# A fused attention and recurrence block: the query split and the gate's scaling move to GpSimd, the gated product reads PSUM, queries are scaled at their projection, and pieces are re-timed

## The chip, the cores and the metric

One Trainium2 chip; the program runs on one of its cores. The metric is the device time of one execution in microseconds (us), the median of several runs. Engines are named as the profile names them: PE is TensorE (PEld its weight loads), DVE VectorE, ACT ScalarE, POOL GpSimd, SP the queue that issues the transfers.

## The reference

2048 tokens of 1024 channels, float32. Eight attention heads of 128 channels with a forget bias, and a gated recurrence beside them; both are normed, gated and multiplied by one output matrix, then a second gate is added. The attention branch, which the change touches, is:

```python
xn = rmsnorm(h, pre_gain[i])
z = xn @ w_in[i]
q, k, v, fl, g_attn, x_lru, g_lru = jnp.split(z, SPLIT_POINTS, axis=-1)
# per head, causal, c = cumsum(log_sigmoid(fl + b_f)):
s = jnp.einsum('bhqd,bhkd->bhqk', qi, k) * HEAD_DIM ** -0.5
s = s + (ci[:, :, :, None] - c[:, :, None, :])
w = jax.nn.softmax(s, axis=-1)            # masked above the diagonal
o = jnp.einsum('bhqk,bhkd->bhqd', w, v)
y_attn = rmsnorm(o_attn, attn_out_gain[i]) * jax.nn.silu(g_attn)
...
mix = jnp.concatenate([y_attn, y_lru], axis=-1) @ w_out[i]
```

## The kernel before

Every product of matrices is made of three matmuls (`mm3`, lines 65 to 70): each operand is split into a high half, rounded to the matmul's format, and a low half, the rest; high x high, high x low and low x high are summed in a PSUM bank. `split` (line 47) makes the halves: ACT or another engine copies, DVE or POOL subtracts.

There are three stages. In the first the projections are made and written to memory: keys `kT_d`, queries `qT_d`, values `v_d`, gates `gT_d`. `plan_pair` makes two 512-row blocks of a pair of projections with seven products of half the size; `sum_` adds each finished bank to a running tile on DVE (line 375), and the last sums of a key and query unit (kind "k") are the queries, named "o" and "t2".

The second stage is attention. Its order is written out by hand: time is cut in slots, and `before` and `after` hold the work that is issued at the begin and the end of a slot; `at(before, slot, f)` puts it there, and each engine works through its own instructions in that order. A unit is a head h and a group g of 512 query rows. Group g has 4g + 4 key blocks and takes as many slots, so that a head has 4 + 8 + 12 + 16 = 40 slots; `t0[n]` is the first slot of unit n, and the boundary between two heads lies at t0 of a group 0. In a slot TensorE issues, in this order: the scores of a later unit (into one of three PSUM banks `sbank`), the value products of three slots before (`AHEAD`; into `obank`), and the transposes of one key block's probabilities (into `tbank`). In the last three slots of a unit a key block touches only some of the four query blocks, so the transposes and value products there are narrower.

What the other engines do for it:

- DVE reads a score bank, adds the forget bias (`bias`, or `dg` at the diagonal) and takes the running minimum `m` (line 1298); the bank is free when this is done. ACT takes the exponential (line 1307).
- ACT and DVE split the transposed probabilities into `th` and `tl` (lines 54 and 60).
- The next unit's queries are loaded into `qf` and split into `qh` (ACT, line 1235) and `ql` (DVE, line 1237) by `split_u`, four to seven slots before its first scores.
- The next head's keys and values come in eight pieces of 512 rows (`kvf`, three buffers), even ones keys, odd ones values: `load_piece` issues the transfer, `split_piece` makes `kh`, `vh` on ACT and `kl`, `vl` on POOL.
- `spread_sums` brings the inverse sums of the exponentials to all partitions (`rb`, line 1363). When a unit's value products are done, `finish_unit` forms `on` = bank x `rb` (line 1367), `gate_unit` forms `gs` = `on` x gate (line 1370), both on DVE, and POOL adds the squares of `on` to `acca` (lines 1377 to 1380).
- POOL also adds the causal mask to `dg` (line 1153) and does chores of the third stage (`make_t`, line 1496; `scale_l`, line 1479).

In the last head the output weights (`wst`) are loaded and split on ACT and POOL as well. The third stage makes the output products.

Of the kernel before, what the change touches and what calls it, by code (L numbers as in the profile page):

```python
# [9 lines left out]
F32 = mybir.dt.float32  # L10
F32R = mybir.dt.float32r
AF = mybir.ActivationFunctionType
ALU = mybir.AluOpType
# [3 lines left out]
P = 128  # L17
# [3 lines left out]
KD = D // P  # L21
# [3 lines left out]
BIG = 3.0e38  # L25
QSCALE = 128.0 ** -0.5
# [12 lines left out]
LOAD, COMBINE, PREP, JOB, MUL, GATE, STORE = range(7)  # L39
# [8 lines left out]
def f32(ap):  # L48
    return ap.bitcast(F32)


def split(nc, src, hi, lo, eh, el):
    if eh == "act":
        nc.scalar.activation(hi, src, AF.Copy)  # L54
    elif eh == "dve":
        nc.vector.tensor_copy(hi, src)
    else:
        nc.gpsimd.tensor_copy(hi, src)
    eng = nc.vector if el == "dve" else nc.gpsimd
    eng.tensor_tensor(out=lo, in0=src, in1=f32(hi), op=ALU.subtract)  # L60


def mm3(nc, out, ws, xs, start, stop):


    wh, wl = ws
    xh, xl = xs
    nc.tensor.matmul(out, lhsT=wh, rhs=xh, start=start, stop=False)  # L68
    nc.tensor.matmul(out, lhsT=wh, rhs=xl, start=False, stop=False)  # L69
    nc.tensor.matmul(out, lhsT=wl, rhs=xh, start=False, stop=stop)  # L70
# [3 lines left out]
def hymba_kernel(ctx: ExitStack, tc: tile.TileContext, x, xT, pT, w_p, w_v, w_o, w_ple, w_pg,  # L74
                 w_gates, vecs, rows, mgrp, out):
    nc = tc.nc
# [37 lines left out]
    rstd_a = const.tile([P, TB], F32, name="rstd_a")  # L114
# [48 lines left out]
    def pool_(stack, name, bufs=1, side="left", space=None):  # L163
        kw = {"side": side} if space is None else {"side": side, "space": space}
        return stack.enter_context(tc.tile_pool(name=name, bufs=bufs, reuse_waits="tile", **kw))


    def scaled_split(q, hi, lo):
        nc.scalar.activation(hi, q, AF.Copy, scale=QSCALE)
        nc.vector.scalar_tensor_tensor(out=lo, in0=q, scalar=QSCALE, in1=f32(hi), op0=ALU.mult, op1=ALU.subtract)  # L170

    p1 = ctx.enter_context(ExitStack())
    ps1 = ctx.enter_context(ExitStack())
    kvA_stack = ctx.enter_context(ExitStack())
# [13 lines left out]
    rs_x = xp.tile([P, TB], F32, name="rs_x")  # L188
    zf = xp.tile([P, NH, TB], F32, name="zf")
    carry = xp.tile([P, NH], F32, name="carry")  # L190
    ps = pool_(ps1, "ps1", 2, space=PSUM)
    pairs_stack = ps1.enter_context(ExitStack())
    wide = [pool_(pairs_stack, "pairs", 3, space=PSUM), None]
# [4 lines left out]
    def bank():  # L198
        return wide[1].tile([P, 512], F32, name="bank", bufs=6)
# [5 lines left out]
    def sbank():  # L205
        return ps.tile([P, 512], F32, name="sbank", bufs=2)

    def ctile():
        return ep.tile([P, 512], F32, name="c", bufs=NC)
# [3 lines left out]
    def plan(slot, phase, f):  # L213


        assert (slot, phase) >= tuple(now), (slot, phase, now)
        order_[0] += 1
        heapq.heappush(calendar.setdefault(slot, []), (phase, order_[0], f))
# [155 lines left out]
    def add(o, x, y):  # L374
        nc.vector.tensor_tensor(out=o, in0=x, in1=y, op=ALU.add)  # L375

    def plan_pair(u, done):


        b, T = u.begin, {}  # L380

        def mul(i):
            T[i] = bank()
            wh, wl, _ = u.ops[i, 0]
            for k in range(4):
                ks = slice(k * P, (k + 1) * P)
                mm3(nc, T[i], (wh[:, ks], wl[:, ks]), (XH[i][:, k], XL[i][:, k]), k == 0, k == 3)

        def copy(name, src):
            T[name] = ctile()  # L390
            nc.scalar.activation(T[name], T[src], AF.Copy)

        def sum_(name, x, y):
            if name not in T:
                T[name] = ctile()
            add(T[name], T[x], T[y])

        for m, i in enumerate(u.order):
            plan(b + m, MUL, lambda i=i: mul(i))

        plan(b + 1, COMBINE, lambda: copy("t1", 0))
        plan(b + 2, COMBINE, lambda: sum_("t2", 2, "t1"))
        plan(b + 3, COMBINE, lambda: sum_("t1", 5, "t1"))
        plan(b + 4, COMBINE, lambda: sum_("t5", 1, "t2"))
        plan(b + 6, COMBINE, lambda: sum_("o", 4, "t5"))
        plan(b + 6, COMBINE, lambda: sum_("t2", 4, "t2"))
        plan(b + 7, COMBINE, lambda: sum_("t5", 3, "t5"))
        plan(b + 7, COMBINE, lambda: sum_("t2", 6, "t2"))
        done(u, 0, 0, T, "t1", b + 3)
        done(u, 1, 1, T, "o", b + 6)  # L410
        done(u, 0, 1, T, "t5", b + 7)
        done(u, 1, 0, T, "t2", b + 7)
# [404 lines left out]
    b = sbank()  # L817
# [128 lines left out]
    for i in range(8):  # L946
        h, c = jobs.pop(0)
# [30 lines left out]
    for i in range(24):  # L978
        h, c = jobs.pop(0)
# [87 lines left out]
    parts_ = {}  # L1067
# [33 lines left out]
    def q_split(g):  # L1101
        qh = kvA_[0].tile([P, 512], F32R, name=f"qh{g}", bufs=1)
        ql = kvA_[0].tile([P, 512], F32R, name=f"ql{g}", bufs=1)
        scaled_split(parts_.pop(("q", g)), qh, ql)
        early_q[g] = qh, ql

    def first_masks():
# [72 lines left out]
    def load_piece(h, n):  # L1180
        c = n // 2
        f = ap.tile([P, 4, P], F32, name="kvf", bufs=3)
        if n % 2 == 0:
            nc.sync.dma_start(out=f.rearrange("p a b -> p (a b)"), in_=kT_d[h, :, c * 512:(c + 1) * 512])
        else:
            nc.sync.dma_start(out=f, in_=v_d[h, :, c * 4:c * 4 + 4])
        pieces[h, n] = f

    def split_piece(h, n):
        if n == 0:  # L1190
            s = Ctx()
            kv = kvB if h % 2 else kvA
            s.kh = kv.tile([P, S], F32R, name="kh")
            s.kl = kv.tile([P, S], F32R, name="kl")
            s.vh, s.vl = {}, {}
            heads[h] = s
        s = heads[h]
        f = pieces.pop((h, n))
        c = n // 2
        if n % 2 == 0:  # L1200
            cs = slice(c * 512, (c + 1) * 512)
            split(nc, f.rearrange("p a b -> p (a b)"), s.kh[:, cs], s.kl[:, cs], "act", "pool")
        else:
            bs, a = slice(c % 2 * 4, c % 2 * 4 + 4), c // 2
            if c % 2 == 0:
                kv = kvB if h % 2 else kvA
                s.vh[a] = kv.tile([P, 8, P], F32R, name=f"vh{a}")
                s.vl[a] = kv.tile([P, 8, P], F32R, name=f"vl{a}")
            split(nc, f, s.vh[a][:, bs], s.vl[a][:, bs], "act", "pool")
# [21 lines left out]
    def split_u(u, part):  # L1231
        if part == 0:
            u.qh = ap.tile([P, 512], F32R, name="qh", bufs=2)
            u.ql = ap.tile([P, 512], F32R, name="ql", bufs=2)
            nc.scalar.activation(u.qh, u.qf, AF.Copy, scale=QSCALE)
        else:
            nc.vector.scalar_tensor_tensor(out=u.ql, in0=u.qf, scalar=QSCALE, in1=f32(u.qh),
                                           op0=ALU.mult, op1=ALU.subtract)

    p1.close()  # L1240
    ps1.close()
# [9 lines left out]
    def load_w(n, k):  # L1251
        w_raw[n, k] = w1s[0].tile([P, 512], F32, name="wst", bufs=3)
        nc.sync.dma_start(out=w_raw[n, k], in_=W_SOURCE[W_ORDER[n]](k))

    def w_high(n, k):
        nc.scalar.activation(WO[n % 2][k][:, :512], w_raw[n, k], AF.Copy)

    def w_low(n, k, eng):
        w = WO[n % 2][k]
        eng.tensor_tensor(out=w[:, 512:], in0=w_raw.pop((n, k)), in1=f32(w[:, :512]), op=ALU.subtract)  # L1260
# [7 lines left out]
    av = pool_(p2, "av", 2)  # L1268
# [98 lines left out]
        nc.vector.tensor_tensor(out=u.on, in0=u.o, in1=u.rb, op=ALU.mult)  # L1367

    def gate_unit(u):
        nc.vector.tensor_tensor(out=u.gs, in0=u.on, in1=u.gs, op=ALU.mult)  # L1370

    def add_squares(h, g, u):
        on = u.on
# [6 lines left out]
            eng.tensor_tensor(out=acca[:, cs], in0=acca[:, cs], in1=on, op=ALU.add)  # L1380

    def load_gate(h, g, u):
        u.gs = av.tile([P, 512], F32, name="gs")
        nc.sync.dma_start(out=u.gs, in_=gT_d[h, :, g * 512:(g + 1) * 512])

    def store_y(h, g, u):
# [4 lines left out]
    t0, t = [], 4  # L1391
# [4 lines left out]
    units = {0: u0, 1: second[0]}  # L1396
    before = {}
    after = {}

    def at(d, slot, f):  # L1400
        d.setdefault(max(slot, 0), []).append(f)
# [23 lines left out]
    for n in range(2, NS):  # L1425
        s0 = t0[n - 1] - LEAD
        lo = max(t0[n - 2] - LEAD, s0 - 8)
# [4 lines left out]
        at(after, sq + 1, lambda n=n: split_u(units[n], 1))  # L1432
        at(after, min(lo + 4, s0 - 1), lambda n=n: mask_u(units[n]))
    for n, (h, g) in enumerate(stages):
        at(before, max(t0[n] - 4, t0[n - 1] + 10) if n else t0[n] + 1, lambda h=h, g=g, n=n: load_gate(h, g, units[n]))
    for p_, a in ((5, 15), (7, 23)):
        at(before, a - 6, lambda p_=p_: load_piece(0, p_))
        at(after, a, lambda p_=p_: split_piece(0, p_))
    for h in range(1, NH):
        base = t0[4 * (h - 1)]  # L1440
        for p_ in range(8):
            a = base + (13, 16, 26, 28, 31, 33, 36, 38)[p_]
            at(before, a - 4, lambda h=h, p_=p_: load_piece(h, p_))
            at(after, a, lambda h=h, p_=p_: split_piece(h, p_))

    def open_w1():
        kvA_stack.close()
# [5 lines left out]
    w1s = []  # L1453
    last0 = t0[4 * (NH - 1)] + AHEAD + 1
    at(before, last0, open_w1)
    for a, (n, k) in zip((0, 2, 3, 5, 6, 8, 9, 11, 23, 26, 29), [(0, k) for k in range(KD)] + [(1, k) for k in range(3)]):
        a += last0
        at(before, a, lambda n=n, k=k: load_w(n, k))
        at(after, a + 4, lambda n=n, k=k: w_high(n, k))
        at(after, a + 4, lambda n=n, k=k: w_low(n, k, nc.gpsimd))  # L1460

    def scales_rows():
        b = psT.tile([P, 512], F32, name="tbank")
# [553 lines left out]
```

## Time and profile before

| | before |
|---|---|
| median of 3 runs | 2071.91 us (2069.89 to 2072.64) |
| profiled execution, its own time | 2074.98 us |
| its span | 2073.2 us |
| attention stage in it | about 1040 to 1592 us |

The span runs from the first to the last instruction; 1.8 us of the execution's time lie around it. Busy time is what an engine spends in instructions. Matmuls overlap in their pipeline, so the distance from one matmul's start to the next says more than their lengths. A bracket behind a row of the timeline gives the idle time before it on its engine and what ended it. L1298 is line 1298 of the kernel.

### The profile page before, as it was taken

What the parts mean: (1) busy time and instruction counts of PE and PEld (TensorE: products, weight loads), DVE (VectorE), ACT (ScalarE), POOL (GpSimd) and SP (SyncE); (2) the same over time, 40 slices, a digit from 0 to 9 for tenths busy, and PEclk for the clock granted to TensorE, in tenths of its full rate; (3) what the DMA queues carried; (4) which work ended last, traced back from release to release, by engine and by line L of the source; (5) the groups of instructions that cost most, each with busy time, mean ns of one, the idle gap of its engine ahead of it and who ended that gap; (6) DMA issues with size and microseconds to landing.
All of it is one profiled execution on the core that took longest, in us unless ns stands there. A gap on an engine that the chain in (4) does not pass through costs nothing.

```text
span 2073.2 us, 31244 instructions
## 1 busy us (share of the span) xinstructions
PE 2057.1 (99%) x10599; PEld 1742.4 (84%) x10599; DVE 1621.7 (78%) x2689; ACT 1151.5 (56%) x1855; POOL 697.0 (34%) x612
## 2 busy tenths in 40 slices
PE   9999999999999999999999999999999999999999
PEld 6988888888988898888888878888888888888887
DVE  8977997696749877986388878888885778776676
ACT  7536665344237776874167767777774344442232
POOL 4333555333013335633135665666642000000000
PEclk9999999999999999999999999999999999999999
DMA  9698898987899888779867767778653887665553
GB/s 346 215 324 296 318 348 307 375 315 282 270 283 277 276 272 293 253 258 324 253 191 236 247 209 216 237 234 241 195 173 124 291 244 231 190 216 181 171 177 117
DMA packets 254675, 518.63 MB, mean 250 GB/s; under 512 B 24866, under 2 KB 91698, under 8 KB 254515
## 3 DMA queue, kind: packets, MB, share of 16 engines
q1 hardware_dynamic: 254368, 516.59, 75.7%
q8 instruction: 83, 1.36, 0.3%
q14 instruction: 78, 0.63, 0.1%
q10 hardware_dynamic: 146, 0.05, 0.0%
HBM read 314.29 MB, written 202.25 MB: 249 GB/s over the span
## 4 chain that ended last, share of the span: by engine, by line
PE 93%; DVE 4%; DMA 1%; issue 1%; ACT 1%; POOL 0%; SPq 0%; DVEq 0%; POOLq 0%; ACTq 0%
PE bank L68 15%; PE bank L70 15%; PE bank L69 15%; PE pbank L70 7%; PE pbank L68 7%; PE pbank L69 7%; PE tbank L1342 5%; PE sbank L68 4%; PE sbank L70 3%; PE sbank L69 3%; PE obank L69 3%; PE obank L70 3%; PE obank L68 3%; PE bank L1884 1%; PE tbank L1361 1%
## 5 line engine op out<-in xcount | busy, mean ns | idle before, releaser
L68 PE MATMUL bank<-XH,op 128*128 128x512 f32 x876 | 342.8, 391 | 0.9 <-DVE u L375 0.9
L70 PE MATMUL bank<-XH,op 128*128 128x512 f32 x876 | 341.4, 390 | 0.0
L69 PE MATMUL bank<-XL,op 128*128 128x512 f32 x876 | 341.4, 390 | 0.0
L375 DVE TENSOR_TENSOR c<-bank,c 128x512 f32<-128x512 f32 x280 | 186.3, 684 | 109.5 <-PE bank L70 103.0
L60 DVE TENSOR_TENSOR tl<-tbank,th 128x512 fp32r<-128x512 f32 (+1 forms) x320 | 192.0, 606 | 78.7 <-ACT th L54 77.0
L54 ACT ACTIVATE th<-tbank 128x512 fp32r<-128x512 f32 (+1 forms) x320 | 167.4, 530 | 108.7 <-PE tbank L1342 102.3
L68 PEld LDWEIGHTS bank<-XH,op 128*128 128x128 f32 x876 | 164.6, 188 | 35.1 <-ACT op L297 1.1
L69 PEld LDWEIGHTS bank<-XL,op 128*128 128x128 f32 x876 | 164.6, 188 | 34.4 <-issue 0.5
L70 PEld LDWEIGHTS bank<-XH,op 128*128 128x128 f32 x876 | 164.5, 188 | 34.2
L1307 ACT ACTIVATE pr<-pr,m 128x1024 f32<-128x1024 f32 (+14 forms) x128 | 150.3, 1175 | 36.1 <-DVE m L1298 35.3
L1342 PE MATMUL tbank<-ident,pr 128*128 128x128 f32 x1062 | 167.4, 273 | 0.0
L152 POOL TENSOR_TENSOR rsm<-rs,mhalf 128x1 f32<-128x1 f32 x16 | 8.7, 541 | 435.0 <-DVE rs L151 435.0
L1342 PEld LDWEIGHTS tbank<-ident,pr 128*128 128x128 f32 x1062 | 130.5, 140 | 27.5 <-DVE tl L60 0.3
L68 PE MATMUL sbank<-kh,qh 128*128 128x512 f32 (+3 forms) x320 | 135.3, 423 | 3.5 <-DVE m L1298 3.0
L68 PE MATMUL obank<-th,vh 128*128 128x512 f32 (+1 forms) x320 | 123.4, 386 | 1.8 <-ACT th L54 1.8
L297 ACT ACTIVATE op<-wq 128x512 fp32r<-128x512 f32 (+1 forms) x95 | 59.5, 629 | 111.1 <-PE bank L70 82.4
L69 PE MATMUL obank<-tl,vh 128*128 128x512 f32 (+1 forms) x320 | 117.9, 369 | 0.2 <-DVE tl L60 0.2
L70 PE MATMUL obank<-th,vl 128*128 128x512 f32 (+1 forms) x320 | 116.9, 365 | 0.0
L70 PE MATMUL sbank<-kh,ql 128*128 128x512 f32 (+3 forms) x320 | 115.9, 362 | 0.0
L69 PE MATMUL sbank<-kl,qh 128*128 128x512 f32 (+3 forms) x320 | 115.3, 360 | 0.0
L69 PE MATMUL bank<-XL,wr 128*128 128x512 f32 x244 | 95.1, 390 | 0.0
L68 PE MATMUL bank<-XH,wr 128*128 128x512 f32 x244 | 95.1, 390 | 0.0
(359 smaller groups left out, 5763.8 us busy)
## 6 DMA issues: line engine op xcount, KB each, us to landing
wo_d<-op SPq DMA_DIRECT2D x140, 512.0 KB, 5.3
op<-wo_d SPq DMA_DIRECT2D x79, 512.0 KB, 6.0
wr<-wo_d SPq DMA_DIRECT2D x61, 512.0 KB, 6.2
wq<-in_w_p_dram SPq DMA_DIRECT2D x40, 512.0 KB, 6.1
wst<-wt_d SPq DMA_DIRECT2D x56, 256.0 KB, 3.5
vo_d<-op SPq DMA_DIRECT2D x27, 516.0 KB, 4.3
wst<-in_w_o_dram SPq DMA_DIRECT2D x40, 256.0 KB, 3.2
X<-xr_d SPq DMA_DIRECT2D x32, 257.5 KB, 4.0
```

Source lines behind the costliest of these rows:

```text
L54: nc.scalar.activation(hi, src, AF.Copy)
L60: eng.tensor_tensor(out=lo, in0=src, in1=f32(hi), op=ALU.subtract)
L68: nc.tensor.matmul(out, lhsT=wh, rhs=xh, start=start, stop=False)
L69: nc.tensor.matmul(out, lhsT=wh, rhs=xl, start=False, stop=False)
L70: nc.tensor.matmul(out, lhsT=wl, rhs=xh, start=False, stop=stop)
L152: nc.gpsimd.tensor_tensor(out=o, in0=t, in1=mhalf[:, :n], op=ALU.pow)
L297: nc.scalar.activation(op[:, :n], self.source(i, hf), AF.Copy)
L375: nc.vector.tensor_tensor(out=o, in0=x, in1=y, op=ALU.add)
L1307: nc.scalar.activation(pr[0][:, a:z], pr[0][:, a:z], AF.Exp, bias=m2, scale=-1.0, accum_out=u.rs[:, c:c + 1])
L1342: nc.tensor.transpose(b[:, i * P:(i + 1) * P], u.P[i][:, sb * P:(sb + 1) * P], ident)
L1361: nc.tensor.transpose(b[:, i * P:(i + 1) * P], u.r4[:, i:i + 1].broadcast_to([P, P]), ident)
L1884: nc.tensor.transpose(b[:, k * P:(k + 1) * P], u.xt[:, kk * P:(kk + 1) * P], ident)
```

## The change

- The scale 128^-0.5 is put on the queries at their projection: the last sum of a query half becomes one DVE instruction that adds, multiplies and takes a minimum into `least`, a column that nothing reads. The later splits are then plain copies and subtractions.
- `split_u` makes `ql` on POOL instead of DVE.
- `gate_unit` multiplies the bank itself by the gate tile; that tile was multiplied by `rb` on POOL before (`scale_gate`), two slots after the unit's begin (four for the first unit). `gs` has three buffers instead of two, and its load moves to four slots ahead of the unit.
- Pieces 6 and 7 are split at slots 44 and 48 of a head's count instead of 36 and 38, and pieces are loaded up to seven slots ahead, not before the slot after the split of the piece that had the buffer.
- The output weights of the last head are loaded three slots ahead of their split instead of four, and most are split two to four slots later.

```diff
-    def scaled_split(q, hi, lo):
-        nc.scalar.activation(hi, q, AF.Copy, scale=QSCALE)
-        nc.vector.scalar_tensor_tensor(out=lo, in0=q, scalar=QSCALE, in1=f32(hi), op0=ALU.mult, op1=ALU.subtract)
...
+    least = rstd_a[:, :1]
...
-        plan(b + 6, COMBINE, lambda: sum_("o", 4, "t5"))
+        def last(name, x, y):
+            if u.kind != "k":
+                return sum_(name, x, y)
+            if name not in T:
+                T[name] = ctile()
+            nc.vector.tensor_tensor_reduce(out=T[name], in0=T[x], in1=T[y], scale=QSCALE, scalar=BIG,
+                                           op0=ALU.add, op1=ALU.min, accum_out=least)
+
+        plan(b + 6, COMBINE, lambda: last("o", 4, "t5"))
         plan(b + 6, COMBINE, lambda: sum_("t2", 4, "t2"))
         plan(b + 7, COMBINE, lambda: sum_("t5", 3, "t5"))
-        plan(b + 7, COMBINE, lambda: sum_("t2", 6, "t2"))
+        plan(b + 7, COMBINE, lambda: last("t2", 6, "t2"))
...
-        scaled_split(parts_.pop(("q", g)), qh, ql)
+        split(nc, parts_.pop(("q", g)), qh, ql, "act", "dve")
...
-            nc.scalar.activation(u.qh, u.qf, AF.Copy, scale=QSCALE)
+            nc.scalar.activation(u.qh, u.qf, AF.Copy)
         else:
-            nc.vector.scalar_tensor_tensor(out=u.ql, in0=u.qf, scalar=QSCALE, in1=f32(u.qh),
-                                           op0=ALU.mult, op1=ALU.subtract)
+            nc.gpsimd.tensor_tensor(out=u.ql, in0=u.qf, in1=f32(u.qh), op=ALU.subtract)
...
     def gate_unit(u):
-        nc.vector.tensor_tensor(out=u.gs, in0=u.on, in1=u.gs, op=ALU.mult)
+        nc.vector.tensor_tensor(out=u.gs, in0=u.o, in1=u.gs, op=ALU.mult)
+
+    def scale_gate(u):
+        nc.gpsimd.tensor_tensor(out=u.gs, in0=u.gs, in1=u.rb, op=ALU.mult)
...
-        u.gs = av.tile([P, 512], F32, name="gs")
+        u.gs = av.tile([P, 512], F32, name="gs", bufs=3)
...
-        at(before, max(t0[n] - 4, t0[n - 1] + 10) if n else t0[n] + 1, lambda h=h, g=g, n=n: load_gate(h, g, units[n]))
+        at(before, t0[n] - (4 if n > 1 else -1), lambda h=h, g=g, n=n: load_gate(h, g, units[n]))
+        at(after, t0[n] + (2 if n else 4), lambda n=n: scale_gate(units[n]))
...
-            a = base + (13, 16, 26, 28, 31, 33, 36, 38)[p_]
-            at(before, a - 4, lambda h=h, p_=p_: load_piece(h, p_))
-            at(after, a, lambda h=h, p_=p_: split_piece(h, p_))
+        places_ = (13, 16, 26, 28, 31, 33, 44, 48)
+        for p_, a in enumerate(places_):
+            at(before, base + max(a - 7, places_[p_ - 3] + 1 if p_ > 2 else 0), lambda h=h, p_=p_: load_piece(h, p_))
+            at(after, base + a, lambda h=h, p_=p_: split_piece(h, p_))
...
-    for a, (n, k) in zip((0, 2, 3, 5, 6, 8, 9, 11, 23, 26, 29), [(0, k) for k in range(KD)] + [(1, k) for k in range(3)]):
+    for a, (n, k) in zip((8, 9, 10, 12, 13, 14, 16, 17, 27, 30, 33), [(0, k) for k in range(KD)] + [(1, k) for k in range(3)]):
         a += last0
-        at(before, a, lambda n=n, k=k: load_w(n, k))
-        at(after, a + 4, lambda n=n, k=k: w_high(n, k))
-        at(after, a + 4, lambda n=n, k=k: w_low(n, k, nc.gpsimd))
+        at(before, a - 3, lambda n=n, k=k: load_w(n, k))
+        at(after, a, lambda n=n, k=k: w_high(n, k))
+        at(after, a, lambda n=n, k=k: w_low(n, k, nc.gpsimd))
```

How this moves instructions is shown at three places. The first is DVE's order at the end of a head, where the scores of the next head's group 1 are read. Before (the score read is the row `pr,m<-sbank`, followed by the read of its minimum, `m`):

```order
L1298 ISA pr,m<-sbank,dg_13572,m 128x256
L1298 ISA m 128x1
L60 TENSOR_TENSOR tl<-tbank,th 128x384
L1237 SCALAR_TENSOR_TENSOR ql<-qf,qh 128x512
L1298 ISA pr,m<-sbank,bias 128x512
L1298 ISA m 128x1
```

The same place now:

```order
L1302 ISA pr,m<-sbank,dg_13590,m 128x256
L1302 ISA m 128x1
L60 TENSOR_TENSOR tl<-tbank,th 128x384
L1302 ISA pr,m<-sbank,bias 128x512
L1302 ISA m 128x1
```

The query's low half no longer stands ahead of the read of the score bank.

The second place is POOL's order over the same stretch: from the last mask of group 1 (`dg`) to the first mask of group 2; `vl` and `kl` are low halves of pieces, `qh` and `kvs` here are chores' tiles. Before:

```order
L1153 TENSOR_TENSOR dg_13578<-dg_13578,cmask 128x128
L60 TENSOR_TENSOR vl_13682<-kvf,vh_13681 128x512
L1496 TENSOR_TENSOR qh_13334<-qh_13334,qh_13332 128x512
L60 TENSOR_TENSOR kl<-kvf,kh 128x512
L60 TENSOR_TENSOR vl_13682<-kvf,vh_13681 128x512
L1479 TENSOR_TENSOR kvs<-kvs,pr_13653 128x512
L1153 TENSOR_TENSOR dg_13734<-dg_13734,cmask 128x128
```

Now:

```order
L1158 TENSOR_TENSOR dg_13596<-dg_13596,cmask 128x128
L60 TENSOR_TENSOR vl_13696<-kvf,vh_13695 128x512
L1504 TENSOR_TENSOR qh_13349<-qh_13349,qh_13347 128x512
L1242 TENSOR_TENSOR ql<-qf,qh 128x512
L1487 TENSOR_TENSOR kvs<-kvs,pr_13667 128x512
L1158 TENSOR_TENSOR dg_13744<-dg_13744,cmask 128x128
```

The splits of pieces 6 and 7 are gone from here, and the query's low half stands in their place.

The third place is DVE's order at the end of a unit. Before:

```order
L1367 TENSOR_TENSOR on<-obank,rb 128x512
L60 TENSOR_TENSOR tl<-tbank,th 128x256
L1370 TENSOR_TENSOR gs<-on,gs 128x512
L1298 ISA pr,m<-sbank,bias 128x512
L1298 ISA m 128x1
```

Now:

```order
L1371 TENSOR_TENSOR on<-obank,rb 128x512
L60 TENSOR_TENSOR tl<-tbank,th 128x256
L1374 TENSOR_TENSOR gs<-obank,gs 128x512
L1302 ISA pr,m<-sbank,bias 128x512
L1302 ISA m 128x1
```

The order is the same; the gated product takes the bank instead of `on`, and the score read still stands behind it.

More of the change, by code (lines that the diff above doesn't have):

```diff
@@ L1440, in hymba_kernel @@
         base = t0[4 * (h - 1)]
-        for p_ in range(8):
-            a = base + (13, 16, 26, 28, 31, 33, 36, 38)[p_]
-            at(before, a - 4, lambda h=h, p_=p_: load_piece(h, p_))
-            at(after, a, lambda h=h, p_=p_: split_piece(h, p_))
+        places_ = (13, 16, 26, 28, 31, 33, 44, 48)
+        for p_, a in enumerate(places_):
+            at(before, base + max(a - 7, places_[p_ - 3] + 1 if p_ > 2 else 0), lambda h=h, p_=p_: load_piece(h, p_))
+            at(after, base + a, lambda h=h, p_=p_: split_piece(h, p_))
     def open_w1():
```

## The prediction

> **What bounds the kernel now.** I read the page first (busy shares, the chain that ended last), then the busy times by stage, then TensorE's waits in the attention stage, then the timeline around each of those waits.
>
> First from the page: the span, the busy line, the chain by engine. Then the stages (start:end in us, length, busy time and count of PE, PEld, DVE, ACT, POOL, granted clock, DMA share, GB/s): projections, attention, output.
>
> ```profile
> span 2073.2 us, 31244 instructions
> PE 2057.1 (99%) x10599; PEld 1742.4 (84%) x10599; DVE 1621.7 (78%) x2689; ACT 1151.5 (56%) x1855; POOL 697.0 (34%) x612
> ...
> PE 93%; DVE 4%; DMA 1%; issue 1%; ACT 1%; POOL 0%; SPq 0%; DVEq 0%; POOLq 0%; ACTq 0%
> ```
>
> ```profile
> 100.00:1040.00 940.00, 939.12 (x4629) 799.39 (x4628) 726.90 (x1046) 521.85 (x764) 345.72 (x246) 1.00 0.87 295
> 1040.00:1592.00 552.00, 546.49 (x3228) 467.04 (x3227) 452.78 (x1092) 391.11 (x727) 298.25 (x311) 1.00 0.68 209
> 1592.00:2073.00 481.00, 476.30 (x2200) 395.42 (x2198) 352.58 (x448) 176.28 (x267) 12.83 (x18) 1.00 0.63 204
> ```
>
> TensorE is the bound everywhere, at full granted clock (1.00), and the change takes no matmul away. So only TensorE's gaps can be won: 940.00 - 939.12 = 0.9 us in the projections, 552.00 - 546.49 = 5.5 us in attention. DVE's 453 us and POOL's 298 us of 552 are no bound by themselves. What TensorE waited for in attention (us in total, times, longest), and the same for the weight loads that run ahead of the matmuls:
>
> ```profile
> PE sbank L68 <- DVE m L1298: 3.0, 6, 0.8
> PE obank L68 <- ACT th L54: 1.8, 1, 1.8
> PE obank L69 <- DVE tl L60: 0.2, 1, 0.2
> ```
>
> ```profile
> PEld sbank L68 <- DVE m L1298: 11.3, 25, 1.2
> ```
>
> Two kinds of wait, then: a score bank (sbank) that DVE has not read yet, and transposed weights (th) that ACT brings late.
>
> **The five waits at the boundary between heads.** Five of the six sbank waits stand at one place, the last slots of a head, where transposes and value products are narrow, so TensorE asks for score banks fastest. The first fence is one of them (start, length), the second the same place two heads from the end, where nothing is lost:
>
> ```profile
> 1306.80 1.28 POOL L60 TENSOR_TENSOR kl<-kvf,kh 128x512 fp32r<-128x512 f32 x1
> ...
> 1307.18 1.45 DVE L1237 SCALAR_TENSOR_TENSOR ql<-qf,qh 128x512 fp32r<-128x512 f32 x1
> ...
> 1308.40 0.40 PE L70 MATMUL sbank<-kh,ql 128*128 128x512 f32 x1
> 1308.56 0.68 DVE L1298 CUSTOM_DVE_ANT_0 pr<-sbank,bias 128x512 f32<-128x512 f32 x1
> ...
> 1309.29 0.44 PE L68 MATMUL sbank<-kh,qh 128*128 128x384 f32 x1 [0.49 <-DVE m L1298]
> ```
>
> ```profile
> 1505.31 0.68 DVE L1237 SCALAR_TENSOR_TENSOR ql<-qf,qh 128x512 fp32r<-128x512 f32 x1
> ...
> 1506.53 0.40 PE L70 MATMUL sbank<-kh,ql 128*128 128x512 f32 x1
> ...
> 1506.76 0.33 PE L68 MATMUL sbank<-kh,qh 128*128 128x384 f32 x1
> ```
>
> The query's low half (ql) takes 0.68 us when POOL is idle and 1.45 us when POOL splits a key piece beside it. In the long case the read of the bank starts at 1308.56, ends about 1309.2, and TensorE starts at 1309.29, 0.89 us after its last matmul; undisturbed, the step is 1506.76 - 1506.53 = 0.23. Lost: 0.66 us, of which the row calls 0.49 idle; 0.17 hides in the modelled end of the matmul before. Of the 3.0 us of sbank waits 0.23 belong to the gate (below), so the boundaries have 2.8 us idle, and 2.8 + 5 x 0.17 = 3.6 us lost.
>
> The change takes ql off DVE altogether (30 times). Without it the bank's read at this boundary starts at 1307.2 and ends at 1307.9, before the 1308.63 at which TensorE could go on: all 3.6 us go. POOL now does ql, and it must be there before the scores that use it. At this boundary ACT's high half and TensorE's use, in an early product of the unit:
>
> ```profile
> 1304.76 0.62 ACT L1235 ACTIVATE qh<-qf 128x512 fp32r<-128x512 f32 x1
> ...
> 1313.53 0.39 PE L70 MATMUL sbank<-kh,ql 128*128 128x512 f32 x1
> ```
>
> with this price of a POOL subtraction of the same shape (count, busy us, mean ns):
>
> ```profile
> L60 POOL TENSOR_TENSOR kl<-kvf,kh 128x512 fp32r<-128x512 f32 x28 | 37.1, 1326 | 92.3 <-ACT kh L54 71.3 <-DMA dg<-nb_d 14.3 <-DMA bias<-nb_d 6.7
> ```
>
> ql can start at 1305.4 and, even behind one other POOL instruction, ends at 1305.4 + 2 x 1.3 = 1308.0, 5.5 us before its use. The moved pieces 6 and 7 also clear POOL's queue just here, and with them two ACT splits.
>
> **The gate.** The gating product (gs) read two SBUF tiles; now it reads the PSUM bank and one SBUF tile, as the product `on` already does. Durations are min/median/max ns; then busy us and mean of gs and ql.
>
> ```profile
> L1370 DVE TENSOR_TENSOR gs<-on,gs x32: 679/962/1791, 1059.8 to 1592.7; 128x512 f32<-128x512 f32 x32
> L1367 DVE TENSOR_TENSOR on<-obank,rb x32: 678/685/691, 1058.6 to 1592.0; 128x512 f32<-128x512 f32 x32
> ```
>
> ```profile
> L1370 DVE TENSOR_TENSOR gs<-on,gs 128x512 f32<-128x512 f32 x32 | 36.7, 1145 | 0.0
> L1237 DVE SCALAR_TENSOR_TENSOR ql<-qf,qh 128x512 fp32r<-128x512 f32 x30 | 24.2, 806 | 0.0
> ```
>
> gs spreads from 679 to 1791, `on` from 678 to 691, in a stage in which POOL is busy 54% of the time (298 of 552 us). I price the new gs like `on`: 32 x (1145 - 685) = 14.7 us off DVE; with ql 24.2 + 14.7 = 38.9 us. Little of the gs part reaches TensorE, since most gates have slack. One place shows it:
>
> ```profile
> 1059.76 1.29 DVE L1370 TENSOR_TENSOR gs<-on,gs 128x512 f32<-128x512 f32 x1
> ...
> 1061.71 0.50 PE L68 MATMUL sbank<-kh,qh 128*128 128x512 f32 x1 [0.23 <-DVE m L1298]
> ```
>
> 0.23 idle and 0.17 hidden, 0.4 us. The other 19 of the 25 late weight loads leave no idle time in the rows; a few stand behind a long gate. Bounds 0 and 19 x 0.1 = 1.9 us (0.1 an estimate: less than the hidden 0.17); I take 1.0.
>
> Behind the moved product stand two new waits. DVE's gs waits for POOL's scaling of the gate, and the score reads queue behind it. The tightest unit is a head's first: the sums' row rb lands on ACT, and gs follows four slots later.
>
> ```profile
> 1315.64 0.59 ACT L1363 ACTIVATE rb<-tbank 128x512 f32<-128x512 f32 x1
> ...
> 1325.58 0.95 DVE L1370 TENSOR_TENSOR gs<-on,gs 128x512 f32<-128x512 f32 x1
> ```
>
> 1325.58 - (1315.64 + 0.59) - 1.3 = 8.0 us of slack. The gate's load is moved ahead of t0 on SP (three buffers instead of two), so it has landed by then. I price this wait at 0. POOL as a whole: (30 + 32) x 1.3 = 81 us more, 298 + 81 = 379 of 552 us, 69%.
>
> [...]
>
> **The pieces.** The largest single wait, at 1237.91, came from a late piece:
>
> ```profile
> 1232.35 1.29 POOL L60 TENSOR_TENSOR kl<-kvf,kh 128x512 fp32r<-128x512 f32 x1
> 1233.67 0.32 SPq L1186 DMA_DIRECT2D kvf<-v_d x1
> ...
> 1235.83 0.28 PE L70 MATMUL sbank<-kh,ql 128*128 128x256 f32 x1
> 1236.75 0.63 ACT L54 ACTIVATE vh<-kvf 128x512 fp32r<-128x512 f32 x1 [3.45 <-DMA kvf<-v_d]
> 1237.91 0.50 PE L68 MATMUL obank<-th,vh 128*128 128x512 f32 x1 [1.81 <-ACT th L54]
> ```
>
> Piece 7 reuses the buffer of piece 4; SP could issue it only when POOL had split piece 4 (1233.64), ACT then waited 3.45 us at the head of its queue for the landing, the th behind it were late, and TensorE lost 2.0 + 0.2 us. Pieces now load up to seven slots ahead instead of four, and 6 and 7 go to slots 44 and 48, past the crowded place; this accident should go. It happened at one of seven heads here, so I do not take that it happens in each execution.
>
> **Small costs.** Head 0's first moved ql had 0.15 us to spare:
>
> ```profile
> 1045.80 0.69 DVE L1237 SCALAR_TENSOR_TENSOR ql<-qf,qh 128x512 fp32r<-128x512 f32 x1
> ...
> 1046.64 0.41 PE L70 MATMUL sbank<-kh,ql 128*128 128x512 f32 x1
> ```
>
> On POOL it ends at 1045.8 + 1.3 = 1047.1: TensorE waits 0.4 us, once. In the projections 32 additions (684 ns) become a scaled add with a minimum that nobody reads, priced like the score read of the same shape (0.68 us above) plus its accumulator read:
>
> ```profile
> L375 DVE TENSOR_TENSOR c<-bank,c 128x512 f32<-128x512 f32 x280 | 186.3, 684 | 109.5 <-PE bank L70 103.0
> ...
> L1298 DVE DVE_READ_ACCUMULATOR2_ANT m<- 128x1 f32 x316 | 26.0, 82 | 0.0
> ```
>
> 32 x 0.08 = 2.6 us of DVE, which waits 103 us for TensorE there: 0 (at worst, uncovered, 2.6). The output weights' loads and splits in the last head shift by two to four slots with the same count; their cover is the three slots by which transposes run ahead of value products: 0, at worst one accident of 2 us as above.
>
> **The sum.** Against the profiled execution: 2074.98 - 3.6 - 0.4 - 1.0 - 2.2 + 0.4 = 2068.2. That execution is 3.1 us above the median of the runs, 2071.91, and its accident is most of that; for a median run I count a third of it, 0.7: 2071.91 - 3.6 - 0.4 - 1.0 - 0.7 + 0.4 = 2066.6 us, 0.26% less. A measurement of this kernel can tell about 0.2% (4.1 us, so 2067.8) from no change.
>
> **The rivals.**
> *Half the gain.* The boundary waits shrink but late loads come at new places: piece 5 now waits for the buffer of piece 2, one slot after its split, and the first output weights are loaded three slots ahead of their split, with three buffers. For it: one such accident exists. Against it: leads grow elsewhere. Only 3.6 + 0.4 kept, and 1.5 us of new waits on average: 2071.91 - 4.0 + 1.5 = 2069.4.
> *Nothing is gained.* POOL's new work stretches DVE's reads after all (each by up to 1.45 - 0.68 = 0.77 us), and the boundaries lose as before: 2071.91 - 0.4 = 2071.5. Against it: `on` at 678 to 691. [...]
> *Slower.* DVE waits at gs for POOL's scaling. Place: a head's first unit; POOL works in order and sits behind masks whose bias rows are still in flight (14.3 us of such waits stand in the kl row). It decides once POOL's lag passes the 8.0 us of slack; a lag of 9 us costs about 1 us at each of eight heads, and with the score reads queued behind, 2071.91 - 3.6 + 8 x 1.5 = 2080. Against it: POOL's idle time is mostly waiting for ACT, so it is ahead, not behind.
>
> **How the numbers follow.** Forecast 0.55, half 0.22, nothing 0.15, slower 0.08. The forecast's own range is 2064 to 2068. Low end: all of it with the accident in every run and no first wait, 2071.91 - 3.6 - 0.4 - 1.9 - 2.2 = 2063.8. High end 2071.0, over the half gain and part of the third case, which leaves out the slower case, most of nothing gained and a few hundredths below. Faster by over 0.2%: most of the forecast and a little of the half, 0.56; slower 0.08; the rest, 0.36, within.
>
> **What the profile of the changed kernel would show.** Right: gs at about 685 with a narrow spread, no ql on DVE, no sbank wait at the boundaries, DVE's busy time near 1621.7 - 38.9 + 2.6 = 1585 us and POOL's near 697 + 81 = 778, TensorE's gaps in attention under 2 us instead of 5.5. Wrong: waits of DVE's gs for POOL, of TensorE for POOL's ql after head 0, or of ACT for a landing piece or output weight.

## The result: 0.94% slower

The changed kernel takes 2091.07 us (median of 4 runs, 2086.55 to 2094.91) against 2071.61 us for the kernel before (4 runs). The ratio is 1.0094, 95% interval [1.0073, 1.0115]: slower, where 2066.6 was forecast. The profiled execution took 2091.03 us.

The page of the changed kernel, the lines that answer to the first fence of the prediction, then the projections and attention by the same columns (the attention stage now ends at about 1608 instead of 1592; the row stops at 1600, and the eight us behind it add no gap):

```profile
span 2089.3 us, 31358 instructions
PE 2060.5 (99%) x10599; PEld 1747.1 (84%) x10599; DVE 1597.5 (76%) x2691; ACT 1152.0 (55%) x1855; POOL 763.2 (37%) x674
...
PE 91%; DMA 3%; DVE 3%; issue 1%; ACT 1%; SPq 1%; POOL 1%; DVEq 0%; ACTq 0%; POOLq 0%
```

```profile
100.00:1040.00 940.00, 939.12 (x4626) 798.75 (x4625) 729.52 (x1078) 521.73 (x764) 344.48 (x245) 1.00 0.87 295
1040.00:1600.00 560.00, 541.41 (x3183) 464.71 (x3182) 422.81 (x1060) 388.98 (x722) 364.64 (x373) 0.99 0.66 205
```

The projections are as they were, to 0.01 us of TensorE. The loss lies in attention: TensorE's gaps there went from 5.5 us in 552 to 560.00 - 541.41 = 18.6 in 560, and the granted clock from 1.00 to 0.99. DVE did become lighter and POOL heavier (1597.5 us for a forecast of 1585, 763.2 for 778). What TensorE waited for, then the wait that appears behind it on ACT, and SP's:

```profile
PE sbank L68 <- DVE m L1302: 17.1, 8, 4.0
...
PE sbank L70 <- POOL ql L1242: 0.4, 1, 0.4
```

```profile
ACT qh L1240 <- DMA qf<-qT_d: 29.3, 10, 5.6
```

```profile
SPq L1191 <- POOL kl L60: 45.8, 7, 7.8
```

The same two rows of the kernel before:

```profile
ACT qh L1235 <- DMA qf<-qT_d: 0.9, 1, 0.9
```

```profile
SPq L1186 <- POOL kl L60: 27.0, 13, 3.7
```

The wait on score banks is still DVE's by name (3.0 us before, 17.1 now; of these 15.4 stand at the seven boundaries and 1.69 at head 0's first gate), but DVE no longer makes ql there. At the boundaries it stands behind ACT, which stands behind a query that lands late: 0.9 us before, 29.3 now. One head shows the chain. First SP's transfers and the two engines that release them in the kernel before, from ACT's high half of piece 2 (`kh`) to the load of the next head's group 2 query (`qf`):

```profile
1287.62 0.38 SPq L1222 DMA_DIRECT2D bias<-nb_d  x1
...
1288.05 2.63 SPq L1228 DMA_DIRECT2D dg<-nb_d  x4
...
1292.38 0.64 ACT L54 ACTIVATE kh<-kvf 128x512 fp32r<-128x512 f32 x1
...
1293.10 1.29 POOL L60 TENSOR_TENSOR kl<-kvf,kh 128x512 fp32r<-128x512 f32 x1 [6.72 <-ACT kh L54]
...
1294.41 0.32 SPq L1186 DMA_DIRECT2D kvf<-v_d  x1
...
1295.33 0.61 SPq L1216 DMA_DIRECT2D qf<-qT_d  x1
```

Now the same head in the changed kernel, down to TensorE's wait:

```profile
1299.38 0.60 ACT L1367 ACTIVATE rb<-tbank 128x512 f32<-128x512 f32 x1
...
1300.06 1.30 POOL L1377 TENSOR_TENSOR gs<-gs,rb 128x512 f32<-128x512 f32 x1 [5.26 <-ACT rb L1367]
...
1300.85 0.63 ACT L54 ACTIVATE kh<-kvf 128x512 fp32r<-128x512 f32 x1
...
1301.55 1.30 POOL L60 TENSOR_TENSOR kl<-kvf,kh 128x512 fp32r<-128x512 f32 x1 [0.19 <-ACT kh L54]
...
1302.87 0.32 SPq L1191 DMA_DIRECT2D kvf<-v_d  x1
...
1303.76 0.38 SPq L1227 DMA_DIRECT2D bias<-nb_d  x1
...
1304.19 1.99 SPq L1233 DMA_DIRECT2D dg<-nb_d  x4
...
1306.71 2.35 SPq L1221 DMA_DIRECT2D qf<-qT_d  x1
...
1316.11 0.63 ACT L1240 ACTIVATE qh<-qf 128x512 fp32r<-128x512 f32 x1 [2.90 <-DMA qf<-qT_d]
...
1317.15 0.56 DVE L60 TENSOR_TENSOR tl<-tbank,th 128x384 fp32r<-128x384 f32 x1 [2.01 <-ACT th L54]
1317.62 0.68 DVE L1302 CUSTOM_DVE_ANT_0 pr<-sbank,bias 128x512 f32<-128x512 f32 x1
...
1318.37 0.45 PE L68 MATMUL sbank<-kh,qh 128*128 128x384 f32 x1 [1.23 <-DVE m L1302]
```

In both kernels piece 5's load (`kvf<-v_d`, the row that follows `kl`) waits on SP for POOL's split of piece 2, and goes out as that split ends (1293.10 + 1.29, 1301.55 + 1.30). What stands behind it differs. Before, the bias rows and the four dg loads had gone out seven us earlier, and the query went 0.92 us after piece 5. Now they come behind the wait, with a store, and the query goes 1306.71 - 1302.87 = 3.84 us after it, 2.92 us later. ACT would have taken the query at 1316.11 - 2.90 = 1313.21, which is 10.34 us after piece 5's load; before, it took it at 1304.76 (a row of the prediction), 10.35 us after, without a wait. So ACT comes to it as before, and the query is late. Two things make its wait: the later issue (2.92 us) and a slower landing (9.3 us after the issue, 6.9 before). Before, the query had landed 2.5 us ahead of its use: 2.92 + 2.4 - 2.5 = 2.8 us, for the 2.90 of the row. Behind it wait th on ACT, tl and the bank's read on DVE, and TensorE. ACT waits for this query at each of seven heads, 2.90 to 5.64 us, 27.1 us of the 29.3. At all seven it also takes longer to land: 7.2 to 11.2 us, 8.6 in the median, where it took 5.6 to 9.7, 6.0 in the median. Everything behind piece 5 now goes out at once; whether that slows the landing, no run shows by itself.

### The profile page after: what moved, and what is told of

Its sections match the earlier page's. It is cut to its first block, busy times and chain, and to the rows that moved or that the text cites. A ratio compares the mean times of both kernels' runs of the same rounds, so it can differ in the third digit from the quotient of the medians.

```text
span 2089.3 us, 31358 instructions
## 1 busy us (share of the span) xinstructions
PE 2060.5 (99%) x10599; PEld 1747.1 (84%) x10599; DVE 1597.5 (76%) x2691; ACT 1152.0 (55%) x1855; POOL 763.2 (37%) x674
## 4 chain that ended last, share of the span: by engine, by line
PE 91%; DMA 3%; DVE 3%; issue 1%; ACT 1%; SPq 1%; POOL 1%; DVEq 0%; ACTq 0%; POOLq 0%
PE bank L70 15%; PE bank L68 15%; PE bank L69 15%; PE pbank L70 7%; PE pbank L68 7%; PE pbank L69 7%; PE tbank L1346 5%; PE sbank L68 3%; PE sbank L70 3%; PE sbank L69 3%; PE obank L69 3%; PE obank L70 3%; PE obank L68 2%; DMA qf<-qT_d 2%; PE bank L1892 1%
## 5 line engine op out<-in xcount | busy, mean ns | idle before, releaser
L372 DVE TENSOR_TENSOR c<-bank,c 128x512 f32<-128x512 f32 x248 | 166.5, 684 | 88.9 <-PE bank L70 78.1
L68 PE MATMUL sbank<-kh,qh 128*128 128x512 f32 (+3 forms) x320 | 136.1, 425 | 17.3 <-DVE m L1302 17.1
```

## The experiments

The theory: piece 5's load, moved from slot 29 to 27 ahead of group 1's bias rows, holds SP's queue, and the query behind it is late. The rivals: POOL holds too much (ql, the scaling and its waits for `rb`), or both together. The medians, and the ratio to the kernel before with its interval (against runs of that kernel made beside each, with medians of 2071.5 to 2072.7 us):

| kernel | us | ratio |
|---|---|---|
| changed, pieces as before | 2067.84 | 0.9983 [0.9973, 0.9993] |
| before, only the pieces changed | 2093.36 | 1.0108 [1.0093, 1.0123] |
| changed, piece 5's load at slot 29 | 2066.53 | 0.9976 [0.9967, 0.9986] |
| changed, scaling behind the split | 2086.49 | 1.0075 [1.0060, 1.0090] |
| changed, piece 5 issued by POOL | 2068.69 | 0.9990 [0.9981, 0.9999] |
| changed, query ahead of piece 5 | 2068.37 | 0.9983 [0.9974, 0.9993] |
| before, only piece 5's load at slot 27 | 2109.92 | 1.0179 [1.0160, 1.0198] |
| before, only pieces 5 to 7 changed | 2093.21 | 1.0100 [1.0082, 1.0118] |
| before, only the gate changed | 2070.44 | 0.9999 [0.9990, 1.0008] |
| before, only ql and the scale changed | 2068.18 | 0.9988 [0.9979, 0.9997] |
| changed, piece 5 at 29, first gate early | 2064.72 | 0.9969 [0.9957, 0.9981] |

**The pieces undone.** The loop over the pieces as it was:

```diff
-        places_ = (13, 16, 26, 28, 31, 33, 44, 48)
...
+            a = base + (13, 16, 26, 28, 31, 33, 36, 38)[p_]
+            at(before, a - 4, lambda h=h, p_=p_: load_piece(h, p_))
```

> The changed kernel with the pieces of the next head's keys and values loaded and split in the slots of the kernel before; ql and the gate's scaling stay on GpSimd. Theory (the place of piece 5's load on SP): the load no longer stands ahead of group 1's bias rows, group 2's query and the store, so SP's waits behind a piece fall from 45.8 us to under 30 and ACT's wait of qh for the query's landing from 29.3 us to under 3, and the time falls from 2091 to 2066 to 2070 us. Rival (GpSimd now holds too much: ql, the scaling and its 34.6 us of waits for rb): the pieces' slots hardly matter, 2083 us or more. Rival (both are needed, the scaling's wait lies ahead of the split on GpSimd whatever the load's slot): 2073 to 2080 us.

Measured 2067.84 us; qh waits once for a query, 1.0 us, and SP 32.7 us in all behind kl (the forecast of under 30 was a little off: that wait alone does no harm). The loss sits in the pieces; ql and the scaling on POOL are kept here and cost nothing.

**The pieces alone.** The opposite edit, on the kernel before:

```diff
-            a = base + (13, 16, 26, 28, 31, 33, 36, 38)[p_]
-            at(before, a - 4, lambda h=h, p_=p_: load_piece(h, p_))
...
+        places_ = (13, 16, 26, 28, 31, 33, 44, 48)
...
+            at(before, base + max(a - 7, places_[p_ - 3] + 1 if p_ > 2 else 0), ...
```

> The kernel before with only the pieces' loads and splits in the slots of the changed kernel. Theory (place of piece 5's load): the whole loss comes back without the rest of the change, 2085 to 2092 us, with ACT's qh waiting some 25 us for the query. Rival (GpSimd): no loss, 2069 to 2073 us. Rival (both are needed: without the scaling's wait of 5 us ahead of it, GpSimd splits piece 2 earlier, and SP is held 5 us less): 2072 to 2078 us, qh waiting under 8 us.

Measured 2093.36 us, the whole loss and no less (a little over the 2085 to 2092 that I gave), with qh waiting 23.1 us. POOL has neither ql nor the scaling here, so both rivals fall.

**One load.** In the changed kernel only piece 5's load moves back behind the bias rows:

```diff
-            at(before, base + max(a - 7, places_[p_ - 3] + 1 if p_ > 2 else 0), ...
+            at(before, base + max(a - 7, 29 if p_ == 5 else places_[p_ - 3] + 1 if p_ > 2 else 0), ...
```

> The changed kernel with one load in each head two slots later: piece 5's, from slot 27 to 29, behind group 1's bias rows; the other seven pieces stay where the change put them. Theory: this one load carries the loss, 2066 to 2070 us, qh's wait for the query under 4 us. Rival (the other early loads, of pieces 0 to 4, 6 and 7, crowd the queues as well): 2075 to 2085 us. Rival (GpSimd): 2085 us or more.

Measured 2066.53 us. One load of eight, two slots, is worth 24.5 us. Its trace, of an execution of 2069.11 us, has one wait on a score bank that DVE has not read and one of ACT for a query, both in head 0:

```profile
PE sbank L68 <- DVE m L1302: 1.6, 1, 1.6
```

```profile
ACT qh L1240 <- DMA qf<-qT_d: 2.4, 1, 2.4
```

**The scaling behind the split.** At group 3 POOL's scaling stands directly ahead of piece 2's split and waits there for `rb`, 34.6 us at eight places. Here it goes one slot later:

```diff
-        at(after, t0[n] + (2 if n else 4), lambda n=n: scale_gate(units[n]))
+        at(after, t0[n] + (3 if n % 4 == 3 else 2 if n else 4), lambda n=n: scale_gate(units[n]))
```

> The changed kernel with group 3's scaling of the gate on GpSimd one slot later, so that the split of piece 2 goes ahead of it and doesn't wait behind its wait for rb; the pieces' slots stay as changed. If the wait for rb on GpSimd is the half of the chain that counts: the split is 5 us earlier, SP is freed from piece 5's load 5 us earlier, and the time is 2068 to 2076 us. If the place of the load alone counts, whatever holds the split: 2084 us or more, SP's wait behind the split still over 30 us of 45.8.

Measured 2086.49 us, an interval that overlaps the changed kernel's; SP still waits 45.1 us. The same head in its timeline says why:

```profile
1294.11 0.60 ACT L1367 ACTIVATE rb<-tbank 128x512 f32<-128x512 f32 x1
...
1295.57 0.63 ACT L54 ACTIVATE kh<-kvf 128x512 fp32r<-128x512 f32 x1
...
1296.27 1.29 POOL L60 TENSOR_TENSOR kl<-kvf,kh 128x512 fp32r<-128x512 f32 x1 [6.75 <-ACT kh L54]
...
1297.60 0.32 SPq L1191 DMA_DIRECT2D kvf<-v_d  x1
```

ACT makes rb first and kh 1.46 us later (1.47 in the changed kernel), and the split starts 0.70 us after the start of kh in both. To take away a wait of 5.3 us that stands ahead of a wait that ends later brings the split nothing; the wait just changes its name in the list from rb to kh. The 4.6 us between the medians are not clear of noise; this trace has two of the slow stretches of the last section, that of the changed kernel four, at 1.5 us or more each.

**Another issuer.** Piece 5's load keeps slot and buffer, but POOL issues it, directly behind its own split:

```diff
-            nc.sync.dma_start(out=f, in_=v_d[h, :, c * 4:c * 4 + 4])
+            (nc.gpsimd if h and n == 5 else nc.sync).dma_start(out=f, in_=v_d[h, :, c * 4:c * 4 + 4])
```

> The changed kernel with one edit: piece 5's load is issued from GpSimd's queue instead of SP's, in the same slot and into the same buffer. GpSimd splits piece 2 itself just before, so the load stands behind nothing that waits, and the bias rows, the store and the query's load on SP no longer stand behind it. Theory (head of the line on SP): the loss goes though slot and buffer stay as changed, 2066 to 2071 us, ACT's qh waits under 5 us in all for the query. Rival (the load is simply late for its buffer, and its transfer takes the DMA engines that the query needs): 2080 us or more.

Measured 2068.69 us, 22.4 less than the changed kernel: the load's time and traffic do little harm, its place in SP's order does the rest. ACT now waits 6.7 us in all for pieces of values, but TensorE's waits for th come to only 1.1 us. The row itself is only 0.32 us on SP; what the other issuer saves is the wait ahead of it, 45.8 us at seven heads, and the lateness of what stands behind it. The rows above show this wait for SP: piece 5's load goes out at 1302.87, the split that it waits for ends at 1301.55 + 1.30 = 1302.85, and everything behind it waits too.

**The query ahead.** The pieces stay as changed; only the query of group 2 is loaded at slot 27 instead of 31, so that SP issues it ahead of piece 5:

```diff
-        at(before, lo - (6 if n % 4 == 2 else 4), lambda n=n: do_load_q(n))
+        at(before, lo - (10 if n % 4 == 2 else 4), lambda n=n: do_load_q(n))
```

> The changed kernel with the pieces as changed and only the query of each head's group 2 loaded four slots earlier, slot 27 instead of 31, so that SP issues it ahead of piece 5's waiting load; bias rows and dg loads stay behind that load. If the query's lateness carries the loss: 2066 to 2071 us, qh's wait for it under 5 us, though SP still waits some 45 us behind the split of piece 2. If the bias rows' and dg loads' lateness counts as well (GpSimd's masks wait 59.9 us for dg in the changed kernel): 2074 to 2086 us, with the score reads waiting for a mask.

Measured 2068.37 us, though SP waits much as before and the bias rows and dg loads are as late. ACT's wait, 9.7 us, is more than the 5 I allowed, but none of it stands at a group 2: all five waits are for the query of a group 3, and little reaches TensorE (one sbank wait of 1.2 us):

```profile
SPq L1191 <- POOL kl L60: 38.5, 7, 7.4
```

```profile
ACT qh L1240 <- DMA qf<-qT_d: 9.7, 5, 2.7
```

So the query carries the loss; that POOL's masks wait 55.3 us for dg (59.9 in the changed kernel, 53.2 in the kernel before) does not show in the time.

**Piece 5 alone, a miss.** On the kernel before, its load at slot 27 and nothing else:

```diff
-            at(before, a - 4, lambda h=h, p_=p_: load_piece(h, p_))
+            at(before, a - (6 if p_ == 5 else 4), lambda h=h, p_=p_: load_piece(h, p_))
```

> The kernel before with one edit: piece 5's load at slot 27 instead of 29, all other pieces, the gate and ql as they were. Theory: SP then holds the bias rows, four dg loads, the store and the query of group 2 behind this load's wait for the split of piece 2, and the loss comes back from this one load, 2085 to 2093 us, qh's wait for the query over 18 us. Rival (the other early pieces are needed too, one load alone only shifts the order): 2075 to 2083 us. No effect: 2071 to 2073 us.

Measured 2109.92 us (2103.34 to 2113.20), worse than any theory had it. One load is enough for the loss, but 17 us more came with it. ACT's order at a boundary of this kernel:

```profile
1245.90 0.64 ACT L1235 ACTIVATE qh<-qf 128x512 fp32r<-128x512 f32 x1 [3.17 <-DMA qf<-qT_d]
...
1248.25 0.63 ACT L54 ACTIVATE kh<-kvf 128x512 fp32r<-128x512 f32 x1 [1.72 <-DMA kvf<-kT_d]
1248.79 0.47 ACT L54 ACTIVATE th<-tbank 128x384 fp32r<-128x384 f32 x1
```

Piece 6 is still split in slot 36, directly behind qh; its load is late behind the same wait on SP, so ACT waits twice ahead of th. To test that, pieces 6 and 7 also go where the changed kernel has them:

```diff
-            a = base + (13, 16, 26, 28, 31, 33, 36, 38)[p_]
-            at(before, a - (6 if p_ == 5 else 4), ...
+            a = base + (13, 16, 26, 28, 31, 33, 44, 48)[p_]
+            at(before, a - (4, 4, 4, 4, 4, 6, 7, 7)[p_], ...
```

> The kernel before with piece 5's load at slot 27 as in the run that took 2110 us, and pieces 6 and 7 loaded and split where the changed kernel has them (loads at 37 and 41, splits at 44 and 48). In that run ACT's split of piece 6 stands in slot 36 directly behind qh and waits up to 1.7 us for its own load, which is late behind the same wait. Theory (the 17 us above the run with all pieces moved are piece 6's split behind the late query): 2088 to 2096 us, no wait of kh for a piece. Rival (pieces 0 to 4, eight slots ahead in the changed kernel, saved something there): 2100 us or more.

Measured 2093.21 us, as with all pieces moved. The early loads of pieces 0 to 4 change nothing that shows, and moving pieces 6 and 7 away from qh takes back 17 us of what piece 5 alone brings (no wait of kh for a piece is left, and TensorE's waits on score banks fall from 26.8 to 17.0 us); the changed kernel has both. The two profiled executions are 2103.34 - 2093.56 = 9.8 us apart, just by these waits. The other three runs with piece 5 alone are longer still, at a mean granted clock of 0.989 to 0.990 where the profiled one had 0.995.

**The gate alone and ql alone.** The two other parts, each on the kernel before. The gate, with the three buffers and the load's new slot:

```diff
-        nc.vector.tensor_tensor(out=u.gs, in0=u.on, in1=u.gs, op=ALU.mult)
+        nc.vector.tensor_tensor(out=u.gs, in0=u.o, in1=u.gs, op=ALU.mult)
...
+        at(after, t0[n] + (2 if n else 4), lambda n=n: scale_gate(units[n]))
```

> The kernel before with only the gate's part: the gate is read from PSUM, GpSimd multiplies it by the inverse sums, three buffers. As the prediction priced it: 1.4 us less, 2070.4 us, which a comparison can hardly tell from 2071.9. Rival (DVE waits for GpSimd's scaling at head 0's first group, seen as 1.9 us in the changed kernel's order): 2072 to 2074 us. Rival (each head's scaling holds the split behind rb and so SP): 2075 us or more.

The query's low half, with the scale at the projection:

```diff
-            nc.vector.scalar_tensor_tensor(out=u.ql, in0=u.qf, scalar=QSCALE, in1=f32(u.qh),
-                                           op0=ALU.mult, op1=ALU.subtract)
+            nc.gpsimd.tensor_tensor(out=u.ql, in0=u.qf, in1=f32(u.qh), op=ALU.subtract)
```

> The kernel before with only the query's part: queries scaled at their projection, ql on GpSimd. As the prediction priced it: 3.6 us of waits at head boundaries go and 0.4 us comes at the first ql, 2068.7 us. Rival (GpSimd's ql stretches DVE's reads, no gain): 2071 to 2072 us. Rival (the accident of late piece 7, about 2 us, comes or goes with it): 2067 to 2074 us, seen as ACT's wait of vh before the split of piece 7.

Measured for the gate: 2070.44 us, no difference that shows. The profiled execution took 2074.37 us, 3.9 above that median. What it loses stands at one place, head 0's first unit, where POOL's scaling comes late and DVE's gs, the bank's read and TensorE wait for it (the first row names ACT's th, but the gate's load, issued at 1050.20, lands 11.3 us later, just then). How much of this the other runs have, no trace tells:

```profile
1061.61 1.26 POOL L1373 TENSOR_TENSOR gs<-gs,rb 128x512 f32<-128x512 f32 x1 [9.26 <-ACT th L54]
...
1062.90 0.69 DVE L1370 TENSOR_TENSOR gs<-obank,gs 128x512 f32<-128x512 f32 x1 [3.80 <-POOL gs L1373]
...
1064.26 0.50 PE L68 MATMUL sbank<-kh,qh 128*128 128x512 f32 x1 [3.38 <-DVE m L1298]
```

The query's part: 2068.18 us, forecast 2068.7. One wait of 0.3 us on a score bank is left in its trace. This bears out the price of 3.6 us for the boundary waits, as far as an interval of 0.6 to 4.4 us gained can.

**A better version.** Piece 5's load at slot 29, and head 0's first gate loaded at slot 1 instead of 5, since the scaling there waits 4.6 us for that load in the trace with piece 5 moved alone:

```diff
-        at(before, t0[n] - (4 if n > 1 else -1), lambda h=h, g=g, n=n: load_gate(h, g, units[n]))
+        at(before, t0[n] - (4 if n > 1 else -1 if n else 3), lambda h=h, g=g, n=n: load_gate(h, g, units[n]))
```

> The changed kernel with piece 5's load at slot 29 and, new, head 0's first gate loaded four slots earlier (slot 1 instead of 5). In the kernel with piece 5's load moved alone, GpSimd's scaling waits 4.6 us there for that load, DVE's gate 1.9 us for the scaling, and TensorE 1.6 us for the score reads behind. Theory: these go, 1.6 to 1.9 us less than 2066.5, so 2064.7 us. Rival (the load goes ahead of others on SP and delays a query or a piece instead): 2066 us or more.

Measured 2064.72 us, 0.31% less than before, faster than both kernels. The gate's step of 1.8 us against the run with piece 5 alone lies inside the two intervals; in the traces it shows, since that run's one sbank wait of 1.6 us is gone, and TensorE's matmuls wait only this in attention:

```profile
PE obank L69 <- DVE tl L60: 0.5, 2, 0.3
PE sbank L70 <- POOL ql L1242: 0.4, 1, 0.4
```

## Why the prediction was wrong, step by step

- *The five boundary waits, -3.6 us: borne out.* With piece 5 put back TensorE has no sbank wait at a boundary left, and ql alone gave 2068.18 for 2068.7, within the interval above.
- *The first ql on POOL, +0.4 us: right*, to the digit, in every run that has it.
- *The gated product priced like `on`, 685 ns: right.* It takes 677 to 693 ns, where it took 679 to 1791:

```profile
L1374 DVE TENSOR_TENSOR gs<-obank,gs x32: 677/681/693, 1060.9 to 1608.7; 128x512 f32<-128x512 f32 x32
```

  The rival by which POOL's new work stretches DVE's reads and nothing is gained did not come: of the score reads, those with `bias` alone take 547 to 692 ns, 680 in the median (before 545 to 691, 679 in the median), DVE's product takes 693 at most, and ql alone on POOL brought 0.6 to 4.4 us. But that the 0.4 and 1.0 us which I took for the gate reach TensorE is not shown: the gate alone made no difference that could be told. What I got wrong is its load. I took it to be moved ahead of the unit everywhere, but at head 0's first unit the change leaves it one slot behind the unit's begin. It lands late there, and the scaling's wait, priced at 0, makes TensorE wait about 1.6 us. The slower rival had this wait of DVE for POOL, but for another reason and at eight heads; it occurs at one.
- *The scale at the projections, 0: right.* 939.12 us of 940 in both.
- *The pieces: the step that failed.* I counted the change there only as a cure ("this accident should go"), and gave the new wait of piece 5 to the rival "half the gain", at 1.5 us. It costs 2091.07 - 2066.53 = 24.5 us. The place was named rightly ("piece 5 now waits for the buffer of piece 2, one slot after its split"), but I asked what piece 5 itself loses by its wait, which is nothing (ACT never waits for a piece in the changed kernel's trace), and not what SP issues behind it. So the signs of being wrong list ACT's wait for a landing piece; what came was its wait for a landing query, 29.3 us. Part of the price was in the trace of before: bias and dg take 0.38 + 2.63 us to issue, and the queries of group 2 landed only 0.0 to 3.2 us ahead of their use, so that three us of delay makes ACT wait at nearly all heads. The other part was not: at the seven heads these queries now also take 8.6 us to land in the median instead of 6.0.
- *The sum* without that step came out: the changed kernel with piece 5's load two slots later takes 2066.53 us, the forecast was 2066.6. That it agrees to 0.1 us is in part luck: no run shows the 1.4 us for the gate or the 0.7 us for the accident, and the wait at the first gate, priced at 0, lies in that time (2064.72 us without it).

## What to carry to other kernels

When a load is moved ahead on a queue, as piece 5's was on SP, find the wait at its head (45.8 us at seven heads here) and price what is issued behind it by each transfer's slack from landing to use (0.0 to 3.2 us for the queries of group 2), those that are needed soon above all. Look at the landing of what is let out together, too: here these queries took 8.6 us to land in the median instead of 6.0. The load whose buffer came free late did no such harm behind the urgent ones (2066.53 us), nor issued by the engine that frees the buffer (2068.69 us). And when a wait is taken away, look at what the same instruction would wait for next: behind POOL's wait of 5.3 us for rb stood one for kh, 6.75 us in its row, that ended later.

## What the runs showed of the hardware

In the changed kernel four of TensorE's eight waits on a score bank were followed by a lower granted clock, so that they cost more than their length. After the 3.97 us wait at 1250.47 the granted clock (third column from the right) was 0.85 and then 0.50 for 2.8 us, and the distance between two 512-wide matmuls was 0.43 us instead of 0.23:

```profile
1240.00:1246.00 6.00, 6.00 (x38) 5.20 (x37) 2.96 (x7) 2.08 (x4) 2.33 (x5) 1.00 0.76 210
...
1250.00:1252.00 2.00, 1.53 (x6) 1.28 (x7) 1.76 (x6) 1.11 (x3) 1.52 (x3) 0.85 0.69 122
1252.00:1254.80 2.80, 2.80 (x8) 2.19 (x7) 1.75 (x8) 1.63 (x5) 0.83 (x2) 0.50 0.81 263
```

```profile
1245.87 0.40 PE L69 MATMUL sbank<-kl,qh 128*128 128x512 f32 x1
...
1246.10 0.40 PE L70 MATMUL sbank<-kh,ql 128*128 128x512 f32 x1
...
1250.47 0.44 PE L68 MATMUL sbank<-kh,qh 128*128 128x384 f32 x1 [3.97 <-DVE m L1302]
...
1253.16 0.63 PE L70 MATMUL sbank<-kh,ql 128*128 128x512 f32 x1
...
1253.59 0.63 PE L68 MATMUL sbank<-kh,qh 128*128 128x512 f32 x1
```

The first two us are at 1.00 until 1251.25, at 0.84 in the next quarter of a us and at 0.50 from 1251.50 on, so their 0.85 means 0.6 us at 0.50; with the 2.8 us behind them the slow stretch is 3.4 us long. Of the eight such waits in that trace four were followed by one (1.69, 2.26, 2.80 and 3.97 us long), four were not (1.23 to 2.13 us). The seven at boundaries can be compared, since TensorE's order is the same there: the 50th matmul after the wait starts 9.92 to 9.98 us behind it with a slow stretch, and 8.41 us without, so that a stretch gives away 1.5 to 1.6 us beside the wait itself. The length of a wait does not tell which are followed: one of 1.69 us was, one of 2.13 us was not. What sets a stretch off, no run shows.

With this the loss adds up. The profiled execution of the changed kernel is 2089.3 - 2067.3 = 22.0 us longer than that with piece 5's load two slots later. Its waits on score banks are 17.1 - 1.6 = 15.5 us longer, the prediction's 0.17 us hidden at each of seven boundaries make 1.2, and four slow stretches instead of one some 4.6: 21.3 us.

That the stretches also make the changed kernel's runs spread (8.4 us, against 2.8 in the kernel before) fits the clocks on record: the mean granted clock was 0.998 in the fastest of its runs, 2086.55 us, and 0.995 or 0.996 in the other three.
